# GLA over a whole token group: attention laid out late, by pairs of heads, value rows stored over the values

## The chip, the cores and the metric

The kernel is one launch on one core of a Trainium2 chip. The metric is the device time of that launch in microseconds (us), lower is better. The engines that matter are TensorE (PE, with its weight loads listed as PEld), VectorE (DVE), ScalarE (ACT), GpSimd (POOL) and SyncE (SP, which issues the DMAs). Each engine works through its own instructions strictly in the order in which they stand in the program.

## The reference, cut to what matters

A two-layer decoder trunk runs over 1072 tokens: 16 meta tokens, 8 samples of 4 tokens, and a prompt of 1024. Each layer projects its input once, feeds four mixers of 256 columns each (gated DeltaNet, HGRN2, GLA, retention), projects their concatenation out, normalises, and runs a SwiGLU block. GLA, which the change is about, has 4 heads with 32 key columns and 64 value columns. Per chunk, with `b` the cumulative sum of the log gates:

```python
dec = _masked_exp(b[:, :, None] - b[:, None, :], incl)
att = jnp.einsum('bthk,bshk,btshk->bhts', q, k, dec)
o = (jnp.einsum('bthk,bhkv->bthv', q * jnp.exp(b), s)
     + jnp.einsum('bhts,bshv->bthv', att, v))
s_new = (jnp.exp(b_last)[..., None] * s
         + jnp.einsum('bshk,bshv->bhkv', k * jnp.exp(b_last[:, None] - b), v))
```

HGRN2 uses the same function with 64 key columns. Inputs and outputs are float32.

## The kernel before, in words

Tokens are split into three groups (`GROUPS`): 304 tokens (48 of the lead and two tiles of 128), 384 and 384. A layer has three stages: the input stage (projection of the input, with the four mixers beside it), the output projection, and the feed-forward block.

No order is written by hand. `Kern.run` is a list scheduler that runs while the program is built: a main thread yields the projections, four worker threads yield the mixers' work, and at each step the operation that its cost model places first is emitted. What one thread holds in memory therefore moves the work of all others. Big projections are matmuls of a 128x128 weight tile on 288 to 512 columns, from the tensor R, three for each product. Mixers use small matmuls on parts of the 128x128 array (32x32, 64x64 and so on) from the tensors H and P; each worker has an arena of 3072 columns for its intermediates, two of them in P and two in H. An input of a mixer (`in_begin`) is allocated before its projection and freed by the mixer; when memory is short the main thread waits.

The mixers take tasks from one queue: both DeltaNet pairs for the three groups, then GLA for the three groups, then HGRN2, then retention. A task goes through units (`task_units`). For DeltaNet, HGRN2 and retention these are the lead and the two tiles of group 0, and the three tiles of groups 1 and 2 in one unit. For GLA `HALVES` cuts groups 1 and 2 into a unit of two tiles and one of one tile.

One unit of GLA or HGRN2 is `gated`. It builds the attention matrix level by level (64 and 32 tokens apart, then the levels inside 32: "s8", "s2", "s1" for GLA). A level takes exponentials of differences of `b` (DVE, ACT), small matmuls into a pair of PSUM banks, and copies or predicated copies out. Levels 64 and 32 write into the full attention `at` (128 columns for each head and tile), the inner ones into `ac` (32 columns for each head and tile), whose blocks are copied onto the diagonal of `at` at the end. Then come the rows of keys and values (PE transposes), and `states_and_out`: the state update, the output, and `norm_out`, which normalises with two matmuls of `head_mean` and stores or splits the result. HGRN2 has two heads, so one pair; GLA has two pairs. At the end of a layer's mixers the output projection begins (128x304 or 128x288 matmuls for group 0, 128x512 for groups 1 and 2).

Of the kernel before, what the change touches and what calls it, by code (L numbers as in the profile page):

```python
# [434 lines left out]
class Kern:  # L435
# [1095 lines left out]
    def gated(self, A, l, u, q, k, vs, b, es, K, first, low, upper, S, S0, bo_out, names, sf, spent):  # L1531

        c0, nb, bl = u
        n = nb * bl
# [4 lines left out]
        if lead:  # L1539
            at = A.alloc(H * 48)  # L1540
            yield self.zero(at)
            dst, mrows = at.r("p (h t) -> p h t", h=H), 48
        else:
            at = A.alloc(nb * H * 128)
            yield self.zero(at)
            ac = A.alloc(nb * H * 32)
            yield self.zero(ac)
            dst, mrows = ac.r("p (h x) -> p h x", h=H), 128
        a4 = None if lead else at.r("p (h a t) -> p h a t", h=H, t=128)
        for m in list(first) if lead else list(upper) + list(low):  # L1550
            wk = wq = None
            step = 32
            if m in STEPS:
# [25 lines left out]
            for j in range(H // 2):  # L1579
                bp = self.pair()  # L1580
                prods = []
                for hh in range(2):
                    bk = bp.k(hh)
                    h = 2 * j + hh
                    ks, qs = wk[K * h:K * h + K], wq[K * h:K * h + K]
                    ps = []
                    if lead:
                        ps.append((bk[0:48, 0:48], ks[:, 0:48], qs[:, 0:48]))
                    for a in range(0 if lead else nb):
                        o = 128 * a  # L1590
                        if m == 64:
                            ps.append((bk[0:64, 64 * a:64 * a + 64], ks[:, o:o + 64], qs[:, o + 64:o + 128]))
                        elif m == 32:
                            for z in range(2):
                                ps.append((bk[64 * z:64 * z + 32, 32 * a:32 * a + 32],
                                           ks[:, o + 64 * z:o + 64 * z + 32], qs[:, o + 64 * z + 32:o + 64 * z + 64]))
                        else:
                            for z in range(4):
                                y = step * (4 * a + z)
                                ps.append((bk[32 * z:32 * z + 32, step * a:step * a + step],  # L1600
                                           ks[:, o + 32 * z:o + 32 * z + 32], qs[:, y:y + step]))
                    prods.append(ps)

                for ps in zip(*prods):
                    for x in ps:
                        yield self.mm(*x)
                hs = slice(2 * j, 2 * j + 2)
                if m == 64:
                    yield self.copy2(a4[0:64, hs, :, 64:128], bp[0:64, :, 0:64 * nb].r("p h (a t) -> p h a t", a=nb))
                elif m == 32:  # L1610
                    for z in range(2):
                        r = slice(64 * z, 64 * z + 32)
                        yield self.copy2(a4[r, hs, :, 64 * z + 32:64 * z + 64],
                                         bp[r, :, 0:32 * nb].r("p h (a t) -> p h a t", a=nb))
                elif m in STEPS:
                    yield from self.take_stepped(m, [dst[:, x].r("p (a t) -> p a t", t=32) for x in (2 * j, 2 * j + 1)],
                                                 dst[:, hs].r("p h (a t) -> p h a t", t=32), bp, nb)
                else:
                    nm = (m if isinstance(m, str) else f"l{m}") + ("_0" if lead else "")
                    if lead:  # L1620
                        yield self.pred(dst[0:48, hs], self.mk(nm, 48, 2), bp[0:48, :, 0:48])
                    else:
                        yield self.pred(dst[:, hs].r("p h (a t) -> p h a t", t=32), self.mk4(nm, 2, nb),
                                        bp[:, :, 0:32 * nb].r("p h (a t) -> p h a t", a=nb))
                self.drop(bp)
# [4 lines left out]
        if not lead:  # L1630
            for z in range(4):
                r = slice(32 * z, 32 * z + 32)
                yield self.dcopy(a4[r, :, :, 32 * z:32 * z + 32], dst[r].r("p h (a t) -> p h a t", t=32))
            A.free(ac)
        eb = A.alloc(n)
        yield self.act(AF.Exp, eb, b, scale=es)
        qe = A.alloc(n)
        yield self.tt2(qe, q, eb, MUL)
        ke = A.alloc(n)
        if lead:  # L1640
            yield self.tt2(ke.c(0, 16), b[:, 15:16].bc([128, 16]), b[:, 0:16], SUB)
# [4 lines left out]
            yield self.tt2(ke.r("p (a c) -> p a c", c=128), bv[:, :, 127:128].bc([128, nb, 128]), bv, SUB)  # L1646
        yield self.act(AF.Exp, ke, ke, scale=es)
        yield self.tt2(ke, ke, k, MUL)
        kt = A.alloc(nb * 128)
        A.free(b)  # L1650
        yield from self.rows(ke, nb, bl, [lambda x: iter([self.copy2(kt[0:bl], x[0:bl, 0:nb * 128])])])
        A.free(ke)
        vts = [A.alloc(nb * 128) for _ in vs]
        for v, vt in zip(vs, vts):
            yield from self.rows(v, nb, bl, [lambda x: iter([self.copy2(vt[0:bl], x[0:bl, 0:nb * 128])])])
        self.free(*spent)
        yield from self.states_and_out(A, l, u, qe, kt, vts, at, S, S0, eb, None, K, H, bo_out, names, sf)

    def stepped(self, A, name, q, k, b, es, n):

# [60 lines left out]
            yield self.pred(both, self.mk4("diag", 2, nb), src[:, :, :, 0:32])  # L1721
            yield self.pred(both.r("p h a (i u) -> p h a i u", u=2)[:, :, :, :, 1], self.mk4("s1", 2, nb), src[:, :, :, 32:48])

    def states_and_out(self, A, l, u, qe, kt, vts, at, S, S0, eb, gam, K, H, bo_out, names, sf):

        c0, nb, bl = u
        n = nb * bl
# [13 lines left out]
        else:  # L1741
# [2 lines left out]
                    yield self.mm(bu[K * h:K * h + K, 64 * a:64 * a + 64], kt[:, 128 * a + K * h:128 * a + K * h + K],  # L1744
                                  vv(h, a))
            for a in range(nb):
                sc = gam[0] if gam else eb[:, 128 * a + 127:128 * a + 128]
                yield self.stt(S[a + 1], S[a], sc,
                               bu[:, 64 * a:64 * a + 64], MUL, ADD)
            self.drop(bu)  # L1750
# [6 lines left out]
        for j in range(nv):  # L1757
# [10 lines left out]
            for k in range(2):  # L1768
                for a in range(nb):
                    for hh in range(2):  # L1770
                        h = 2 * j + hh
                        o = bo[64 * hh:64 * hh + 64, bl * a:bl * a + bl]
                        x = h * nb + a
                        if k:
                            r = slice(K * h, K * h + K)
                            yield self.mm(o, S[a][r], qe[r, 128 * a:128 * a + 128], False, a == nb - 1)
                        else:
                            yield self.mm(o, vv(h, a), at[:, 128 * x:128 * x + 128], a == 0, False)
            if j == nv - 1:
                A.free(qe, at, *vts)  # L1780
            yield from bo_out(j, bo)
        if lead:
            yield from self.sample_states(A, l, kt, vts, S0, eb, gam, K, H, names)
# [38 lines left out]

    def task_units(self, A, J, g, state):

        units = (HALVES if J.key[1] == "c" else UNITS)[g]
        mid = A.alloc(64) if g and len(units) == 2 else None
        for k, u in enumerate(units):
            ui = k if g == 0 else g + 1
# [106 lines left out]
    def ret(self, A, l, hh, g, J):  # L1935
# [24 lines left out]
        for x in self.task_units(A, J, g, self.i["sr"][l, hh]):  # L1960
# [41 lines left out]

            if u[0] + n == gn:
                self.free(*ins)
            yield from self.states_and_out(A, l, u, qe, kt, [vt], at, S, S0, None, gam, 64, 2, done,
                                           (None, "rs%d%d" % (l, hh)), sf)
        self.flag(("of", l, 6 + hh, g))

# [644 lines left out]
```

## Time and profile before

| what | value |
| --- | --- |
| median of 3 runs | 3169.23 us (3167.81 to 3171.99) |
| the profiled execution's own time | 3172.53 us |
| its span, first to last instruction | 3170.8 us |
| granted TensorE clock, mean | 0.977 |
| PE busy | 3018.0 us, 95% of the span |
| DVE, ACT, POOL busy | 1731.3, 1111.1 and 529.6 us |
| chain that ended last | PE 65%, DVE 9%, ACT 3%, DMA 2%, issue 2% |

A busy PE is not a PE at its peak: matmuls overlap, and their ends are modelled. So the places where PE is idle or works on small matmuls are read from stretches of the trace, and the pace of the big matmuls from a stretch that holds nothing else. The two input stages lie at about 80 to 640 us and 1640 to 2200 us, each followed by its output projection; the feed-forward blocks fill most of the rest. Fp32 matmuls have two records each in the trace, projections one.

### The profile page before, as it was taken

Reading aid. Unit: us, or ns where it says so; the run is one execution under the profiler, and the core shown is the slowest. Engines: PE = TensorE matmul, PEld = TensorE weight load, DVE = VectorE, ACT = ScalarE, POOL = GpSimd, SP = SyncE. Lnnn points to the kernel's source line nnn. Section 1 sums busy time; section 2 is a strip of 40 time slices with the busy share of each in tenths; the row PEclk is TensorE's granted clock in tenths of the full one; section 3 lists DMA queues with packets and bytes.
Section 4 is the critical chain, followed back from the end, with each engine's and each line's share of the span. In section 5 each row is a group of like instructions: output and inputs, shape, how many; then the busy total and the mean of one; then the engine's idle time right before and its main releaser. Section 6 shows DMA issues by size and latency. Waiting matters only on the chain.

```text
span 3170.8 us, 65772 instructions
## 1 busy us (share of the span) xinstructions
PE 3018.0 (95%) x27758; PEld 2733.2 (86%) x27758; DVE 1731.3 (55%) x3978; ACT 1111.1 (35%) x2310; POOL 529.6 (17%) x617
## 2 busy tenths in 40 slices
PE   7999999989999999999999989999999999999996
PEld 5778887878899999999977778879789999999996
DVE  8886668556633333333497856783774333333336
ACT  5454577432411111111264437763433111111113
POOL 3412213010600000000044211230115000000001
PEclk8999999999999999999999999999999999999998
DMA  5310221241111111111033102123511111111112
GB/s 199 110 49 27 66 64 61 90 158 57 60 54 47 47 40 41 53 47 47 34 125 92 48 26 69 62 65 96 177 47 63 41 40 54 47 47 47 47 40 75
DMA packets 121030, 210.94 MB, mean 67 GB/s; under 512 B 32336, under 2 KB 81488, under 8 KB 120608
## 3 DMA queue, kind: packets, MB, share of 16 engines
q1 hardware_dynamic: 120736, 206.75, 19.7%
q8 instruction: 217, 3.56, 0.5%
q14 instruction: 77, 0.63, 0.1%
HBM read 162.28 MB, written 40.04 MB: 64 GB/s over the span
## 4 chain that ended last, share of the span: by engine, by line
PE 65%; DVE 9%; ACT 3%; DMA 2%; issue 2%; POOL 1%; SPq 0%; DVEq 0%; ACTq 0%; POOLq 0%
PE banks L833 63%; DVE H L864 2%; DVE R L864 2%; DVE H L877 1%; PE banks L839 1%; DVE P L864 1%; ACT H L858 1%; DVE H L902 1%; DVE H L1012 1%; ACT R L855 1%; ACT P L858 1%; ACT L645 0%; DMA H<-XR 0%; DMA H<-OF 0%; POOL H L866 0%
## 5 line engine op out<-in xcount | busy, mean ns | idle before, releaser
L833 PE MATMUL banks<-R 128*128 128x384 f32 (+3 forms) x11840 | 2106.8, 334 | 36.7 <-DVE R L864 13.8
L833 PEld LDWEIGHTS banks<-R 128*128 128x128 f32 x11840 | 1939.0, 191 | 103.9 <-DVE R L864 23.1
L864 DVE TENSOR_TENSOR H<-H,banks 128x512 f32<-128x512 f32 (+6 forms) x722 | 407.3, 568 | 534.6 <-PE banks L833 531.8
L864 DVE TENSOR_TENSOR R<-H,R 128x1024 fp32r<-128x1024 f32 (+5 forms) x356 | 347.8, 987 | 444.6 <-ACT R L855 442.2
L855 ACT CAST R<-H 128x1024 fp32r<-128x1024 f32 (+3 forms) x358 | 284.7, 811 | 803.8 <-PE banks L833 712.0
L833 PE MATMUL banks<-R,P 128*128 128x512 f32 x1584 | 371.7, 394 | 0.0
L833 PEld LDWEIGHTS banks<-R,P 128*128 128x128 f32 x1584 | 296.2, 188 | 66.8 <-issue 0.6
L866 POOL TENSOR_TENSOR H<-H 128x256 f32<-128x256 f32 (+10 forms) x267 | 237.3, 903 | 331.0 <-ACT H L858 81.8
L866 POOL TENSOR_TENSOR P<-H,P 128x384 fp32r<-128x384 f32 (+7 forms) x49 | 73.6, 1503 | 1303.6 <-ACT P L855 1283.4
L858 ACT ACTIVATE H<-H 128x384 f32<-128x384 f32 (+11 forms) x455 | 189.7, 434 | 191.0 <-DVE H L1014 78.9
L833 PE MATMUL banks<-H 32*32 32x32 f32 (+15 forms) x6134 | 203.7, 224 | 22.2 <-issue 8.3
L833 PEld LDWEIGHTS banks<-H 32*32 32x32 f32 (+9 forms) x6134 | 146.8, 121 | 79.5 <-issue 42.8
L833 PE MATMUL banks<-P 32*32 32x32 f32 (+10 forms) x5982 | 170.7, 215 | 26.5 <-DVE P L864 12.4
L833 PEld LDWEIGHTS banks<-P 32*32 32x32 f32 (+6 forms) x5982 | 124.2, 118 | 75.7 <-issue 36.9
L855 ACT COPY H<-banks 128x384 f32<-128x384 f32 (+14 forms) x305 | 112.0, 374 | 219.9 <-PE banks L833 176.6
L855 ACT CAST P<-H 128x304 fp32r<-128x304 f32 (+2 forms) x132 | 64.3, 487 | 284.8 <-DVE H L864 284.8
L864 DVE TENSOR_TENSOR H<-H 128x384 f32<-128x384 f32 (+12 forms) x310 | 131.8, 442 | 50.5 <-ACT H L858 28.9
L858 ACT ACTIVATE H<-banks 128x384 f32<-128x384 f32 (+5 forms) x169 | 72.0, 429 | 228.9 <-PE banks L833 223.5
L839 PE MATMUL banks<-H 128*128 128x128 f32 (+3 forms) x639 | 114.0, 302 | 36.1 <-DVE H L902 16.2
L833 PE MATMUL banks<-P,R 128*128 128x304 f32 (+1 forms) x1056 | 147.4, 299 | 0.0
L833 PEld LDWEIGHTS banks<-P,R 128*128 128x128 f32 x1056 | 145.9, 188 | 0.0
L839 PEld LDWEIGHTS banks<-H 128*128 128x128 f32 (+3 forms) x639 | 77.9, 148 | 69.6 <-DVE H L902 19.0
(86 smaller groups left out, 1714.6 us busy)
## 6 DMA issues: line engine op xcount, KB each, us to landing
H<-in_wst SPq DMA_DIRECT2D x208, 512.0 KB, 3.2
XR<-H SPq DMA_DIRECT2D x12, 512.0 KB, 4.2
GF<-H SPq DMA_DIRECT2D x32, 192.0 KB, 2.2
H<-XR SPq DMA_DIRECT2D x4, 1536.0 KB, 6.7
H<-OF SPq DMA_DIRECT2D x28, 192.0 KB, 4.0
H<-XR SPq DMA_DIRECT2D x41, 128.0 KB, 3.0
XR<-H SPq DMA_DIRECT2D x41, 128.0 KB, 1.8
H<-in_xin SPq DMA_DIRECT2D x8, 512.0 KB, 7.6
```

What stands on the lines that cost most here:

```text
L833: return Op("PE", cost, lambda: self.nc.tensor.matmul(out=out.x(), lhsT=lhsT.ap, rhs=rhs.ap, start=start, stop=stop), (lhsT, rhs), (out,), ...
L839: return Op("PE", 0.83 * p + 2.5, lambda: self.nc.tensor.transpose(out=out.x(), in_=in_.ap, identity=i.ap), (in_,), (out,), 20, None, tile ...
L855: fn = lambda: self.nc.scalar.copy(out=out.x(), in_=in_.x())
L858: fn = lambda: self.nc.scalar.activation(out=out.x(), in_=in_.x(), func=f, scale=s, bias=b)
L864: lambda: self.nc.vector.tensor_tensor(out=out.x(), in0=a.x(), in1=b.x(), op=op), (a, b), (out,))
L866: lambda: self.nc.gpsimd.tensor_tensor(out=out.x(), in0=a.x(), in1=b.x(), op=op), (a, b), (out,), 27.0)
L877: lambda: self.nc.vector.scalar_tensor_tensor(out=out.x(), in0=a.x(), scalar=sc, in1=b.x(), op0=op0, op1=op1),
L902: return Op("DVE", 68 + ptr + rate * out.n, lambda: self.nc.vector.tensor_scalar(out=out.x(), in0=a.x(), **kw), rd, (out,))
L1012: yield Op("DVE", 68 + 1.05 * 512, lambda o=o, s=s: nc.vector.bn_stats(out=o, in_=s.x()), (s,), (st,))
```

## The change

GLA uses the same units as the other mixers, so groups 1 and 2 are one unit of three tiles. To fit the arena, the full attention is allocated only after the inner levels, which now run first, and as one tile for each pair of heads; each is freed as soon as its pair is through. For GLA outside the lead, the transposed value rows are written over the values they came from, whose memory is then freed at the end; `eb` shrinks to its last columns and `qe` takes its place. HGRN2 shares `gated`, so its levels change order too; retention only wraps its attention in a list.

```diff
@@ gated
-            at = A.alloc(nb * H * 128)
-            yield self.zero(at)
             ac = A.alloc(nb * H * 32)
             yield self.zero(ac)
             dst, mrows = ac.r("p (h x) -> p h x", h=H), 128
-        a4 = None if lead else at.r("p (h a t) -> p h a t", h=H, t=128)
-        for m in list(first) if lead else list(upper) + list(low):
+        for m in list(first) if lead else list(low) + list(upper):
+            if not lead and m == upper[0]:
+                at = [A.alloc(nb * 256) for _ in range(H // 2)]
+                for x in at:
+                    yield self.zero(x)
+                a4 = [x.r("p (h a t) -> p h a t", h=2, t=128) for x in at]
...
-                yield self.dcopy(a4[r, :, :, 32 * z:32 * z + 32], dst[r].r("p h (a t) -> p h a t", t=32))
+                for j, x in enumerate(a4):
+                    yield self.dcopy(x[r, :, :, 32 * z:32 * z + 32],
+                                     dst[r, 2 * j:2 * j + 2].r("p h (a t) -> p h a t", t=32))
             A.free(ac)
         eb = A.alloc(n)
         yield self.act(AF.Exp, eb, b, scale=es)
-        qe = A.alloc(n)
-        yield self.tt2(qe, q, eb, MUL)
+        if lead:
+            qe = A.alloc(n)
+            yield self.tt2(qe, q, eb, MUL)
+        else:
+            eb, qe = A.alloc(nb), eb
+            yield self.dcopy(eb, qe.r("p (a c) -> p a c", c=128)[:, :, 127])
+            yield self.tt2(qe, q, qe, MUL)
...
-        vts = [A.alloc(nb * 128) for _ in vs]
+        place = not lead and len(vs) > 1
+        vts = vs if place else [A.alloc(nb * 128) for _ in vs]
...
-        self.free(*spent)
+        self.free(*(spent[:-len(vs)] if place else spent))
@@ states_and_out
-                sc = gam[0] if gam else eb[:, 128 * a + 127:128 * a + 128]
+                sc = gam[0] if gam else eb[:, a:a + 1]
...
-                            yield self.mm(o, vv(h, a), at[:, 128 * x:128 * x + 128], a == 0, False)
+                            yield self.mm(o, vv(h, a), at[j][:, 128 * x:128 * x + 128], a == 0, False)
+            A.free(at[j])
             if j == nv - 1:
-                A.free(qe, at, *vts)
+                A.free(qe, *(() if place else vts))
+                if place:
+                    self.free(*spent[-len(vts):])
@@ task_units
-        units = (HALVES if J.key[1] == "c" else UNITS)[g]
+        units = UNITS[g]
```

What this does to the order of PE's instructions is shown at three places. In the rows, `banks` is PSUM, R holds projections and their weights, H and P the mixers' data, and the last numbers are the output's partitions and columns and how many such matmuls stand together.

First, PE in layer 0, at GLA's inner levels (32x48 matmuls). Before, a unit of two tiles, and further down a unit of one tile:

```order
L833 MATMUL banks<-H 32x48 x32
L833 MATMUL banks<-R 128x384 x14
L833 MATMUL banks<-H 32x48 x32
L833 MATMUL banks<-R 128x48 x2
L833 MATMUL banks<-R 128x384 x12
L833 MATMUL banks<-H 32x48 x32
...
L833 MATMUL banks<-P_74 32x48 x16
L833 MATMUL banks<-R 128x304
L833 MATMUL banks<-R 128x384 x18
L833 MATMUL banks<-R 128x48 x2
L833 MATMUL banks<-R 128x384 x13
L833 MATMUL banks<-P_74 32x48 x16
```

Now the same place, with the three tiles of a group in one burst:

```order
L833 MATMUL banks<-H 32x48 x48
L833 MATMUL banks<-R 128x48 x2
L833 MATMUL banks<-R 128x384 x11
L833 MATMUL banks<-H 64x48 x2
L833 MATMUL banks<-H 64x4 x16
L833 MATMUL banks<-R 128x384 x18
L833 MATMUL banks<-H 32x48 x48
L833 MATMUL banks<-R 128x384 x11
L833 MATMUL banks<-R 128x48 x2
L833 MATMUL banks<-R 128x384 x4
L833 MATMUL banks<-H 32x48 x48
```

Bursts of 32 and of 16 have become one of 48, and the separate bursts of 16 are gone from the order further down.

Second, PE in layer 1, where DeltaNet's triangular inverses (32x32) of two workers stand, before GLA. Before:

```order
L833 MATMUL banks<-H 32x32 x12
L833 MATMUL banks<-P_14795 64x64 x48
L833 MATMUL banks<-P_14795 32x32 x16
L833 MATMUL banks<-H 32x32 x24
L833 MATMUL banks<-H 128x128 x6
L833 MATMUL banks<-H,P_14795 128x64
L833 MATMUL banks<-P_14795 32x32 x16
L833 MATMUL banks<-H 32x32 x24
L833 MATMUL banks<-H 64x64 x45
L833 MATMUL banks<-P_14795 32x32 x16
L833 MATMUL banks<-H 32x32 x24
L833 MATMUL banks<-H 64x64 x3
```

Now the same place, by the number of projection matmuls that stand ahead of it:

```order
L833 MATMUL banks<-P_14617 64x64 x48
L833 MATMUL banks<-P_14617 32x32 x8
L833 MATMUL banks<-H 32x32 x24
L833 MATMUL banks<-R 128x304 x8
L833 MATMUL banks<-P_14617 32x32 x8
L833 MATMUL banks<-H 32x32 x24
L833 MATMUL banks<-R 128x304 x6
L833 MATMUL banks<-P_14617 128x128 x4
L833 MATMUL banks<-H 32x32 x24
L833 MATMUL banks<-R 128x304 x6
L833 MATMUL banks<-P_14617 64x64 x32
L833 MATMUL banks<-H 32x32 x24
```

Projection matmuls (R) now stand between the small ones, where before 235 small matmuls stood together.

Third, PE at the end of layer 0's input stage: the last retention unit (64x64 x6 and 64x128 x12 from H, then `head_mean`, 128x384 from R) and the output projection around it. Before:

```order
L839 MATMUL banks<-H 128x128 x6
L833 MATMUL banks<-H 128x128 x6
L833 MATMUL banks<-H 64x64 x6
L833 MATMUL banks<-R 128x512 x14
L833 MATMUL banks<-H 64x128 x12
L833 MATMUL banks<-R 128x512 x7
L833 MATMUL banks<-R 128x384 x2
L833 MATMUL banks<-R 128x512 x11
L833 MATMUL banks<-R 128x384 x2
L833 MATMUL banks<-R 128x512 x4
L833 MATMUL banks<-R 128x304 x48
L833 MATMUL banks<-R 128x512 x72
```

Now:

```order
L833 MATMUL banks<-R 128x304 x48
L833 MATMUL banks<-R 128x512 x18
L839 MATMUL banks<-H 128x128 x6
L833 MATMUL banks<-H 128x128 x6
L833 MATMUL banks<-R 128x512 x3
L833 MATMUL banks<-H 64x64 x6
L833 MATMUL banks<-R 128x512 x6
L833 MATMUL banks<-H 64x128 x12
L833 MATMUL banks<-R 128x512 x7
L833 MATMUL banks<-R 128x384 x2
L833 MATMUL banks<-R 128x512 x11
L833 MATMUL banks<-R 128x384 x2
```

The last unit stood in the first pass of the output projection and now stands in the second, behind its 48 matmuls of group 0. In layer 1 it moved the other way, from the second pass into the first.

## Rows read from the trace of the kernel before

**Rows 1.** The page: span, and each engine's busy time, share, instructions.

```profile
span 3170.8 us, 65772 instructions
PE 3018.0 (95%) x27758; PEld 2733.2 (86%) x27758; DVE 1731.3 (55%) x3978; ACT 1111.1 (35%) x2310; POOL 529.6 (17%) x617
```

**Rows 2.** Windows: length; busy PE, PEld, DVE, ACT, POOL (instructions); PEclk, DMA share, GB/s.

```profile
80.00:640.00 560.00, 527.44 (x8134) 455.60 (x8133) 389.24 (x1143) 304.12 (x699) 131.97 (x200) 0.98 0.22 68
1640.00:2200.00 560.00, 521.53 (x8064) 454.09 (x8064) 381.20 (x1152) 301.12 (x696) 139.29 (x205) 0.97 0.21 65
840.00:1560.00 720.00, 720.00 (x4185) 688.90 (x4185) 250.88 (x369) 122.95 (x190) 57.78 (x39) 1.00 0.13 47
```

**Rows 3.** The chain that ended last (start us, us, what): layer 0's feed-forward block.

```profile
838.59 732.70 PE banks L833 x4266
```

**Rows 4.** Timeline of PE, layer 0: start us, us, instruction, records, [idle].

```profile
307.06 1.32 PE L833 MATMUL banks<-R 128*128 128x384 f32 x6
308.31 0.62 PE L833 MATMUL banks<-P 32*32 32x32 f32 x48
308.86 0.30 PE L833 MATMUL banks<-H 32*48 32x48 f32 x8
309.09 1.33 PE L833 MATMUL banks<-R 128*128 128x384 f32 x6
310.35 0.94 PE L833 MATMUL banks<-P 32*32 32x32 f32 x80
311.21 1.14 PE L833 MATMUL banks<-R 128*128 128x384 f32 x5
```

**Rows 5.** The same view, GLA's inner levels: two tiles, one tile.

```profile
358.10 0.80 PE L833 MATMUL banks<-H 32*32 32x48 f32 x64
428.91 0.37 PE L833 MATMUL banks<-P 32*32 32x48 f32 x32
```

**Rows 6.** Windows as in rows 2, over GLA's units in either layer.

```profile
280.00:520.00 240.00, 225.87 (x3378) 192.42 (x3377) 165.95 (x539) 149.77 (x376) 55.19 (x95) 0.96 0.18 57
1880.00:2080.00 200.00, 194.34 (x2544) 169.15 (x2540) 133.37 (x465) 134.20 (x327) 42.92 (x75) 1.00 0.19 61
```

**Rows 7.** Groups by form: count | busy us, mean ns of one | idle before, releaser.

```profile
L864 DVE TENSOR_TENSOR H<-H 128x384 f32<-128x384 f32 x81 | 46.1, 584 | 18.6 <-DMA H<-H 11.1 <-ACT H L858 4.9 <-PE banks L833 1.3
L864 DVE TENSOR_TENSOR H<-H 128x256 f32<-128x256 f32 x45 | 20.8, 462 | 10.6 <-ACT H L858 5.4 <-PE banks L833 4.8
L864 DVE TENSOR_TENSOR H<-H 128x128 f32<-128x128 f32 x48 | 13.5, 297 | 3.7 <-ACT H L858 3.5
L858 ACT ACTIVATE H<-H 128x384 f32<-128x384 f32 x161 | 81.8, 520 | 32.1 <-DVE H L864 15.0 <-DVE H L877 12.7 <-DVE H L902 1.6
L858 ACT ACTIVATE H<-H 128x256 f32<-128x256 f32 x38 | 15.6, 414 | 6.9 <-DVE H L864 4.0 <-DVE H L907 2.4
L858 ACT ACTIVATE H<-H 128x128 f32<-128x128 f32 x39 | 11.4, 307 | 9.2 <-POOL H L866 4.4 <-DVE H L864 3.0 <-DVE H L907 1.6
L645 ACT ACT_TABLE_LOAD x98 | 125.7, 1283 | 1.7
L927 POOL MEMSET H<- 128x768 f32 x13 | 9.6, 739 | 36.3 <-PE banks L833 36.2
```

**Rows 8.** Layer 1's dense stretch: window; PE's waits (total us, times, longest).

```profile
1800.00:1880.00 80.00, 67.75 (x2096) 58.28 (x2086) 50.01 (x148) 21.85 (x56) 14.46 (x21) 0.96 0.07 20
PE banks L833 <- issue: 7.9, 7, 2.2
```

**Rows 9.** Windows as in rows 2: the ends of the two input stages.

```profile
640.00:720.00 80.00, 66.38 (x421) 55.64 (x420) 49.49 (x97) 31.12 (x66) 14.32 (x13) 0.87 0.47 149
2200.00:2280.00 80.00, 75.68 (x533) 65.48 (x532) 49.84 (x103) 32.81 (x70) 8.65 (x11) 1.00 0.56 183
```

More of the change, by code (lines that the diff above doesn't have):

```diff
@@ L1608, in gated @@
                 if m == 64:
-                    yield self.copy2(a4[0:64, hs, :, 64:128], bp[0:64, :, 0:64 * nb].r("p h (a t) -> p h a t", a=nb))
+                    yield self.copy2(a4[j][0:64, :, :, 64:128], bp[0:64, :, 0:64 * nb].r("p h (a t) -> p h a t", a=nb))
                 elif m == 32:
@@ L1612, in gated @@
                         r = slice(64 * z, 64 * z + 32)
-                        yield self.copy2(a4[r, hs, :, 64 * z + 32:64 * z + 64],
+                        yield self.copy2(a4[j][r, :, :, 64 * z + 32:64 * z + 64],
                                          bp[r, :, 0:32 * nb].r("p h (a t) -> p h a t", a=nb))
@@ L1648, in gated @@
         yield self.tt2(ke, ke, k, MUL)
+        A.free(b)
         kt = A.alloc(nb * 128)
-        A.free(b)
         yield from self.rows(ke, nb, bl, [lambda x: iter([self.copy2(kt[0:bl], x[0:bl, 0:nb * 128])])])
         A.free(ke)
-        vts = [A.alloc(nb * 128) for _ in vs]
+        place = not lead and len(vs) > 1
+        vts = vs if place else [A.alloc(nb * 128) for _ in vs]
         for v, vt in zip(vs, vts):
             yield from self.rows(v, nb, bl, [lambda x: iter([self.copy2(vt[0:bl], x[0:bl, 0:nb * 128])])])
-        self.free(*spent)
-        yield from self.states_and_out(A, l, u, qe, kt, vts, at, S, S0, eb, None, K, H, bo_out, names, sf)
+        self.free(*(spent[:-len(vs)] if place else spent))
+        yield from self.states_and_out(A, l, u, qe, kt, vts, at, S, S0, eb, None, K, H, bo_out, names, sf, place, spent)
     def stepped(self, A, name, q, k, b, es, n):
@@ L1722, in take_stepped, with states_and_out @@
             yield self.pred(both.r("p h a (i u) -> p h a i u", u=2)[:, :, :, :, 1], self.mk4("s1", 2, nb), src[:, :, :, 32:48])
-    def states_and_out(self, A, l, u, qe, kt, vts, at, S, S0, eb, gam, K, H, bo_out, names, sf):
+    def states_and_out(self, A, l, u, qe, kt, vts, at, S, S0, eb, gam, K, H, bo_out, names, sf, place=False, spent=()):
         c0, nb, bl = u
@@ L1772, in states_and_out @@
                         o = bo[64 * hh:64 * hh + 64, bl * a:bl * a + bl]
-                        x = h * nb + a
+                        x = hh * nb + a
                         if k:
@@ L2004, in ret @@
                 self.free(*ins)
-            yield from self.states_and_out(A, l, u, qe, kt, [vt], at, S, S0, None, gam, 64, 2, done,
+            yield from self.states_and_out(A, l, u, qe, kt, [vt], at if lead else [at], S, S0, None, gam, 64, 2, done,
                                            (None, "rs%d%d" % (l, hh)), sf)
```

## The prediction, made before the changed kernel ran

> **What bounds the kernel now.** I read the page first, then the windows of the stages, then the chain. The page says PE: 3018.0 of 3170.8 us busy, DVE 1731.3, ACT 1111.1 [rows 1]. That average hides two kinds of stage. In a feed-forward block PE has no gap at all (720.00 of 720.00 us, clock 1.00), and the chain runs through it as one piece of 4266 matmuls in 732.70 us, 0.172 us each [rows 2, 3]. Nothing of the change lies there. In the two input stages PE is busy 527.44 and 521.53 of 560 us, so idle 32.6 and 38.5 us, and the clock is 0.98 and 0.97 [rows 2]. DVE is busy 389 and 381 us of the 560 (70%), ACT 304 and 301. So even beside the mixers PE is the fullest engine, and its waits are short gaps between bursts, not one engine's backlog. What the change can win is three things: PE's own work, the price of going between big and small matmuls, and a share of these 71 us. The reader is to see that the mixers' work on DVE, ACT and POOL counts only where PE waits for it.
>
> **PE's own work.** The three-tile unit does the same small matmuls for each tile. The rows agree: an inner level of two tiles takes 0.80 us for 64 records and one of one tile 0.37 us for 32 [rows 5], so the pair costs 1.17 us; at the same 12 ns a record, 96 records cost about 1.2. No gain there. What goes is `head_mean`: ten units of more than the lead become six over both layers (five and three in each), with four matmuls each, so 16 matmuls fewer in 21462. Their columns stay (256 + 128 against 384), so I set this at nothing; the work that takes its place is the wider matmul itself, and without that it would be at most 16 times 0.172, 2.8 us.
>
> **Going between big and small.** In the timeline of PE, six projection matmuls between two bursts take 1.25 us from start to start (307.06 to 308.31) and again 1.26 (309.09 to 310.35) [rows 4]. At 0.172 each they would take 1.03, so 0.22 us is lost. The burst behind them: 48 records from 308.31 to 308.86 are 0.55 us, 80 records from 310.35 to 311.21 are 0.86 us, so 9.7 ns a record and 0.08 us fixed [rows 4]. One burst put among projections thus costs 0.30 us beyond its work. Counted over the whole order, runs of matmuls on part of the array fall from 351 to 336, since the one-tile bursts join the two-tile ones: 15 times 0.30, 4.6 us less. The ends are 0, if an idle gap takes the place of each, and 6.9, if each also frees as much again half.
>
> The Trainium skill, TensorEngine Tiling (Array Packing), section "Key Properties", says that changing the tiling mode drains TensorE and gives no price, while its section "PSUM Bottleneck" says that small tiles speed up TensorE but not the evacuation of PSUM, so that the copies out may become the bound. By the first, the 4.6 us above is real; by the second, it is not where the gain is, and the copies decide, which is the second rival below.
>
> **DVE, ACT and POOL.** Counted over the order, and net of what is added: DVE loses 155 instructions, ACT 123 (127 fewer, 4 table loads more), POOL 38. A pair of 256 and 128 columns against one of 384 costs DVE 462 + 297 - 584 = 175 ns more, ACT 414 + 307 - 520 = 201 ns [rows 7]. That is 27 us off DVE and 25.5 off ACT, less 4 x 1.283 = 5.1 us of table loads, so 20. These are beside PE's work nearly everywhere. Where they reach PE is over GLA's units: PE idles 240 - 225.87 = 14.1 us in layer 0 and 200 - 194.34 = 5.7 in layer 1 [rows 6], 19.8 together. GLA's units fall by four in ten, so at most 7.9 us can go if all of that idle time were GLA's. DeltaNet and HGRN2 run there too, so I take half, 4 us; the lower end is 0.
>
> **What is added and moved.** The attention's zeroing on POOL comes late: 0.74 us for 768 columns [rows 7], twice for a GLA unit, once for an HGRN2 unit. It is issued ahead of the chain of level 64 (a subtraction, two exponentials and two products, on 384 columns at 0.52 to 0.58 us each [rows 7], so over 2.5 us), and that hides it. Behind it on POOL stand only shares of the same work, which DVE can take as well. If the cover is gone, 24 such memsets at 0.74 us would be 18 us on the mixers' chain, and PE would see the share that it sees of other mixer time: the 71 us of idle time over 770 us of DVE work in the two stages [rows 2], a tenth, so under 2 us. The 18 small copies of the last column and the doubled diagonal copies are in the net count above. In retention nothing moves but names. The stores and loads of `norm_out` fall by 18 on SP's queue, and nothing is queued behind them that PE waits for. Value rows in the values' place hold the inputs longer, to the end of the output instead of the transposes. But before, all inputs of a group were held until its second unit was through, and that one stood far down (428.91 us for its first inner burst against 358.10 for the first unit's [rows 5]). So I expect memory to come free earlier, not later.
>
> **The new plan around it.** The scheduler places everything after the first GLA task anew. Two places matter.
>
> In layer 1, where two workers' inverses meet, PE idles 80 - 67.75 = 12.3 us in 80, and for 7.9 us of these, 7 times, it waits for nothing that the profile shows ("issue"), in the densest runs of small matmuls [rows 8]. In the order before, the fullest stretch of 20 projection matmuls has 362 small ones beside it there, now 208. In layer 0 the fullest near the first GLA task has 204 now where 100 stood, but the order before has stretches that full in layer 0 as well (236). I take half of the 7.9 us, 4, as gone; the ends are 8 gained and 2 lost.
>
> At the ends of the input stages PE idles 80 - 66.38 = 13.6 us at clock 0.87 in layer 0, and 4.3 us at 1.00 in layer 1 [rows 9]. The order shows that the two layers trade shapes here: layer 0's last retention unit goes from the first pass of the output projection into the second, where layer 1's stood, and layer 1's goes the other way. If the shape makes the gap, one layer gains what the other loses; if the place does (its weights and stores), nothing changes. Either way I set the sum at 0, with ends at one layer's difference: 13.6 - 4.3 = 9.3 us of idle time, plus the clock. A mean of 0.87 is 26% of the 80 us at 1.2 GHz, in which half the work is done, so up to 10.4 us. Together 19.7 us either way.
>
> **Sum.** -4.6 (bursts) - 4 (GLA's gaps) - 4 (dense stretch) + 0 (ends) = -12.6 us. From the profiled execution's 3172.53 us (span 3170.8 and 1.7 around it) this is 3159.9. The median of the runs before is 3.3 us below that execution, so for the median 3156.6, which I give as 3157.
>
> **Rivals.**
>
> *The mixers set the pace.* If PE's gaps came from DVE's backlog, all 27 us of DVE would count beside the 4.6, in place of the two terms of 4: 31.7 us, or 3137 for the median. For it speaks that DVE is 70% busy in the input stages; against it, that PE is at 94% there and DVE never full [rows 2, 6]. Here the skill's page named above would put the bound; the rows show PE fuller than DVE in both of GLA's windows (225.87 against 165.95, 194.34 against 133.37), so it gets little.
>
> *Layer 1 takes layer 0's end, and layer 0 keeps its own.* The head means of the last units then stand among the first output matmuls in both layers, PE waits for them in order, and the clock falls as in rows 9. That costs 19.7 us against the 12.6 gained: 3176. It decides as soon as the new gap is above 12.6 us. For it speaks the trade of shapes; against it, that layer 0's shape goes as well, and with it the most likely cause.
>
> *Nothing comes of it.* The list scheduler fills each freed slot, the joined bursts only move the same waits to the next place, and gaps of 8 us are what two plans of equal worth differ by. Then only part of the 4.6 us shows: 3165 to 3169. For it speaks that all added slack is on engines that are not the bound; against it, that the burst price is paid by PE itself.
>
> **How the numbers follow.** The forecast has a chance of 0.5, with a range of its own from 3148 (both middle terms at their upper ends, 7.9 and 8) to 3165 (both at 0). The faster mixers have 0.13, the worse end of layer 1 0.17, nothing 0.2. A measurement of this kernel tells about 0.2%, 6.3 us, from no change, so faster is below 3162.9 and slower above 3175.6. Faster: 0.43 of the forecast's 0.5, the 0.13, and 0.02 of the nothing case, 0.58. Slower: 0.1 of the 0.17, and some 0.06 from plans that lose elsewhere by as much, 0.16. The rest, 0.26, is the same. The range runs from the faster mixers at 3137 to the worse end with 2 us of the late memsets on top, 3178.
>
> **What would show it.** In the profile after, PE's windows over GLA should have under 16 us of idle time, the busy time of DVE and ACT in the input stages some 10 us less in each layer, the inner levels bursts of 96 records at about 1.2 us, and the waits for "issue" in layer 1's dense stretch half. I am wrong if the feed-forward stretches change, if the two ends of the input stages add up to much more or less than 18 us of idle time, or if the clock in them falls in both layers.

## The result, and the profile after

The changed kernel took 3134.5 us in the median of four executions (3125.1 to 3135.6), the kernel before 3170.6 beside it: a ratio of 0.988, interval 0.986 to 0.990. Six more executions later (e9), on another chip and beside other kernels, gave 0.9902 (0.9880 to 0.9923), some 31 us. So the change is worth 31 to 36 us; forecast were 12.6, and the range missed the first median by 2.5 us.

The page of the changed kernel: span, then busy time, share and instructions of each engine, as in [rows 1].

```profile
span 3132.8 us, 65384 instructions
PE 2993.8 (96%) x27742; PEld 2722.0 (87%) x27742; DVE 1727.6 (55%) x3823; ACT 1098.3 (35%) x2187; POOL 514.7 (16%) x579
```

PE is 24.2 us less busy and 13.8 less idle. DVE issues 155 instructions fewer, as counted, but its busy time falls by 3.7 us only, where 27 were forecast; ACT loses 12.8, POOL 14.9.

Windows of the changed kernel over the stretches of [rows 2, 6, 9], moved with the program in layer 1: length; busy PE, PEld, DVE, ACT, POOL with instructions; PEclk, DMA share, GB/s.

```profile
80.00:640.00 560.00, 526.89 (x8142) 462.31 (x8141) 384.45 (x1064) 291.24 (x634) 125.65 (x178) 0.97 0.22 68
840.00:1560.00 720.00, 720.00 (x4204) 688.73 (x4203) 255.34 (x383) 124.34 (x190) 39.83 (x26) 1.00 0.14 47
280.00:520.00 240.00, 225.92 (x3453) 198.64 (x3451) 167.06 (x461) 147.17 (x325) 52.50 (x80) 0.98 0.19 60
1860.00:2060.00 200.00, 190.88 (x2825) 170.87 (x2823) 142.61 (x399) 136.78 (x286) 42.72 (x65) 1.00 0.21 66
640.00:720.00 80.00, 74.15 (x488) 61.47 (x487) 58.10 (x109) 32.06 (x66) 13.44 (x14) 0.98 0.55 176
2150.00:2230.00 80.00, 71.00 (x508) 63.09 (x505) 46.69 (x98) 33.28 (x71) 10.14 (x10) 0.94 0.52 163
```

The feed-forward block is untouched (720.00 of 720.00 again). Over GLA's units PE idles 14.1 and 9.1 us, 23.2 together, not less than the 19.8 of before, but it gets through more in the same time (3453 matmul records for 3378, 2825 for 2544). The two ends have traded: layer 0's has 5.9 us idle at clock 0.98, layer 1's 9.0 at 0.94.

A window of fixed length holds different work in two kernels. So I cut both programs at the same projections (the head means' matmuls left out, both have 14256): from number 200 to 2200 is layer 0's input stage, to 3000 its end; 7200 to 9200 and to 10000 the same in layer 1. First the kernel before.

```profile
87.80:690.90 603.10, 560.67 (x8346) 485.48 (x8345) 413.53 (x1187) 322.54 (x738) 138.13 (x200) 0.97 0.25 76
690.90:881.20 190.30, 180.51 (x1040) 157.12 (x1040) 120.77 (x201) 61.10 (x113) 58.18 (x46) 0.96 0.21 70
1631.10:2225.30 594.20, 554.19 (x8279) 485.35 (x8279) 400.15 (x1209) 310.51 (x721) 145.14 (x214) 0.97 0.22 67
2225.30:2418.30 193.00, 181.24 (x1121) 156.18 (x1120) 140.09 (x246) 75.19 (x149) 59.83 (x49) 0.98 0.29 98
```

The changed kernel, the same four pieces of work.

```profile
84.20:676.10 591.90, 554.15 (x8336) 486.53 (x8335) 404.69 (x1101) 309.41 (x672) 132.67 (x183) 0.97 0.25 77
676.10:860.50 184.40, 176.33 (x1039) 153.75 (x1039) 126.31 (x209) 61.81 (x114) 56.78 (x46) 0.99 0.23 75
1609.40:2181.90 572.50, 540.67 (x8272) 475.75 (x8272) 401.88 (x1135) 309.47 (x661) 132.15 (x191) 0.99 0.23 69
2181.90:2380.20 198.30, 182.41 (x1119) 158.15 (x1118) 139.49 (x243) 76.04 (x151) 61.54 (x50) 0.97 0.30 96
```

Layer 0's input stage gives 11.2 us (4.7 of them idle time), layer 1's 21.7 (8.2 idle), layer 0's end 5.9, and layer 1's end costs 5.3. PE's busy time also falls, by 6.5 and 13.5 us in the two stages. Part of that is the clock: layer 1's stage was granted 0.97 before and 0.99 after. This part is chance of the two executions shown and not of the change. Over 22 executions of the kernel before the mean granted clock is 0.9819, over the six of e9 0.9827; in the profiled one of before it was 0.977.

To keep chance and plan apart, the table below has, in us and for these four pieces together, the idle time of PE, the time that the clock took (one less the granted clock, times the length), and what is left, PE's own work at full clock. Cut are the kernel before and e1, e3, e12; whole are the changed kernel (mean of its two profiles), e2, e4, e11, all described below.

| us | time | idle | clock | own work |
|---|---|---|---|---|
| before | 1580.5 | 104.0 | 47.8 | 1428.7 |
| changed (two profiles) | 1547.8 | 93.5 | 36.7 | 1417.6 |
| mean of four cut | 1574.6 | 105.6 | 38.8 | 1430.2 |
| mean of four whole | 1554.4 | 97.4 | 39.5 | 1417.5 |

Whole groups have 12.7 us less of PE's own work and 8.2 less idle time, and no better clock.

### The profile page after: what moved, and what is told of

The parts are those of the page before. It is cut to its first block, busy times and chain, and to the rows that moved or that the text cites. A ratio compares the mean times of both kernels' runs of the same rounds, so it can differ in the third digit from the quotient of the medians.

```text
span 3132.8 us, 65384 instructions
## 1 busy us (share of the span) xinstructions
PE 2993.8 (96%) x27742; PEld 2722.0 (87%) x27742; DVE 1727.6 (55%) x3823; ACT 1098.3 (35%) x2187; POOL 514.7 (16%) x579
## 5 line engine op out<-in xcount | busy, mean ns | idle before, releaser
L833 PE MATMUL banks<-R 128*128 128x384 f32 (+2 forms) x11824 | 2094.1, 333 | 26.0 <-DVE H L877 10.0
L864 DVE TENSOR_TENSOR H<-H,banks 128x512 f32<-128x512 f32 (+5 forms) x713 | 403.4, 570 | 528.6 <-PE banks L833 525.6
L864 DVE TENSOR_TENSOR R<-H,R 128x1024 fp32r<-128x1024 f32 (+4 forms) x348 | 348.2, 1011 | 438.5 <-ACT R L855 436.4
L866 POOL TENSOR_TENSOR P<-H,P 128x384 fp32r<-128x384 f32 (+6 forms) x49 | 73.2, 1495 | 1292.3 <-ACT P L855 1282.2
L866 POOL TENSOR_TENSOR H<-H 128x256 f32<-128x256 f32 (+7 forms) x230 | 213.9, 945 | 264.4 <-ACT H L858 83.1
L833 PE MATMUL banks<-H 32*32 32x32 f32 (+13 forms) x5560 | 185.3, 225 | 26.2 <-DVE H L864 11.3
L833 PE MATMUL banks<-P 32*32 32x32 f32 (+12 forms) x6404 | 171.8, 212 | 23.1 <-DVE P L864 8.4
L833 PEld LDWEIGHTS banks<-P 32*32 32x32 f32 (+7 forms) x6404 | 129.3, 117 | 70.5 <-issue 35.8
L855 ACT COPY H<-banks 128x384 f32<-128x384 f32 (+11 forms) x278 | 107.0, 391 | 186.6 <-PE banks L833 155.5
L858 ACT ACTIVATE H<-banks 128x384 f32<-128x384 f32 (+5 forms) x166 | 71.1, 430 | 231.5 <-PE banks L833 224.4
L864 DVE TENSOR_TENSOR H<-H 128x384 f32<-128x384 f32 (+13 forms) x283 | 130.9, 480 | 29.9 <-ACT H L858 17.4
L839 PE MATMUL banks<-H 128*128 128x128 f32 (+4 forms) x636 | 110.0, 295 | 36.9 <-DVE H L902 14.5
```

The costliest lines, as they stand in the source:

```text
L833: return Op("PE", cost, lambda: self.nc.tensor.matmul(out=out.x(), lhsT=lhsT.ap, rhs=rhs.ap, start=start, stop=stop), (lhsT, rhs), (out,), ...
L839: return Op("PE", 0.83 * p + 2.5, lambda: self.nc.tensor.transpose(out=out.x(), in_=in_.ap, identity=i.ap), (in_,), (out,), 20, None, tile ...
L855: fn = lambda: self.nc.scalar.copy(out=out.x(), in_=in_.x())
L858: fn = lambda: self.nc.scalar.activation(out=out.x(), in_=in_.x(), func=f, scale=s, bias=b)
L864: lambda: self.nc.vector.tensor_tensor(out=out.x(), in0=a.x(), in1=b.x(), op=op), (a, b), (out,))
L866: lambda: self.nc.gpsimd.tensor_tensor(out=out.x(), in0=a.x(), in1=b.x(), op=op), (a, b), (out,), 27.0)
```

## The experiments

Fifteen runs follow, of which e9 is the changed kernel again. All ratios are against runs of the kernel before on the same chip, with a 95% interval; 0.1% is 3.2 us.

**Units or layout?** e1 is the changed kernel with GLA's groups cut again.

```diff
-        units = UNITS[g]
+        units = (HALVES if J.key[1] == "c" else UNITS)[g]
```

> The changed kernel with one line put back: GLA's groups 1 and 2 are again a unit of two tiles and one of one tile; late attention by pairs, level order and value rows in place stay. Units theory (the joined bursts and the fewer gaps of whole groups are the gain): most of the 36 us is lost, 3160 to 3172. Layout theory (order of levels, late attention, memory): it stays below 3145. Plan theory (any new order of the scheduler lands some 10 to 20 us up or down): anything from 3130 to 3170, with no relation to the number of bursts.

0.9997 (0.9980 to 1.0014). With the groups cut, all of the gain is gone, so it hangs on the units; the new layout with cut groups is neither gain nor loss. Its page shows what moved between the engines.

```profile
PE 3003.8 (95%) x27758; PEld 2720.6 (86%) x27758; DVE 1747.9 (55%) x4055; ACT 1096.5 (35%) x2301; POOL 529.8 (17%) x611
```

Against before, the layout puts 16.6 us on DVE and takes 14.6 off ACT. The whole groups then take 20.3 off DVE and 15.1 off POOL, and leave ACT as it is. The forecast had put both into one sum.

**The order of the levels.** e2 lets HGRN2 keep its upper levels first (`late` is true for GLA alone).

```diff
-        for m in list(first) if lead else list(low) + list(upper):
+        late = len(vs) > 1
+        for m in list(first) if lead else (list(low) + list(upper) if late else list(upper) + list(low)):
```

> The changed kernel with HGRN2's levels in their old order (64 and 32 first, attention allocated before them); GLA as changed. Units theory: as the changed kernel, 3125 to 3142, since nothing of GLA's units moves. Layout theory: 5 to 15 us of the gain go, 3140 to 3150. Plan theory: 3120 to 3150, by chance.

0.9938 (0.9915 to 0.9961), 3146 us in the median and so outside the 3125 to 3142 of the units theory. Some 12 us of the changed kernel's gain hang on it or on the plan that came with it. Which of the two this run can't tell.

**How far do plans scatter?** e3 and e12 are the kernel before, e4 and e11 the changed one, each with one number of the scheduler altered.

```diff
-HOLD, SLACK = 600.0, 150.0
+HOLD, SLACK = 600.0, 200.0   # e3, e4
+HOLD, SLACK = 650.0, 150.0   # e11, e12
```

> The kernel before with one number of the scheduler changed that does no work of its own (its dislike of going back from small to big matmuls, SLACK, 150 to 200). Units theory: 3160 to 3180. Plan theory: more than 10 us away from 3170, either way; a run at 3150 or below would mean that a redrawn plan alone can give half of the gain.

> The changed kernel with the same number changed (SLACK 150 to 200). Units theory: 3125 to 3145, so that the distance to the kernel before with the same number stays at 25 us or more. Plan theory: more than 10 us away from 3134, either way, and the distance to the kernel before with the same number below 15 us.

> The changed kernel under another plan (the wait that the scheduler puts on a first small matmul 650 for 600). With e2 and e4 a third sample of how far plans of whole groups scatter. If whole groups are worth 0.9% or so by themselves, 0.988 to 0.995; if the changed kernel was a lucky plan, 0.997 to 1.003.

> The kernel before with the same 650 for 600, a sample of how far plans of cut groups scatter, besides e1 and e3 (0.9997 and 1.0000). If the cut itself costs, 0.997 to 1.003 again; if plans scatter by a per cent, anything from 0.990.

Cut groups: e3 1.0000 (0.9988 to 1.0011), e12 0.9969 (0.9953 to 0.9984), with e1 and the kernel itself a mean of 0.9992. Whole groups: e4 0.9915 (0.9888 to 0.9943), e11 0.9922 (0.9893 to 0.9951), with e2 and 0.9902 a mean of 0.9919. None of these plans of whole groups is as slow as the fastest of cut ones, though the intervals of e2 and e12 touch. With the same numbers in the scheduler the distance is 31 us (the kernels themselves, by e9), 27 (e3 to e4) and 15 (e12 to e11). So the units are worth 0.7%, 23 us, by the scatter of four plans of either kind some 8 us more or less. The 8 to 13 us beyond that belong to this pair of plans; why it is a better pair stays open.

**Part of the units.** e6 cuts the second group only, e7 both groups in layer 1 only, e8 cuts both groups into three single tiles.

```diff
+        units = (HALVES if J.key[1] == "c" and g == 1 else UNITS)[g]             # e6
+        units = (HALVES if J.key[1] == "c" and J.key[0] == 1 else UNITS)[g]      # e7
+        units = (THIRDS if J.key[1] == "c" else UNITS)[g]                        # e8
```

> The changed kernel with GLA's second group cut again into two tiles and one, the third left whole. If each joined group is worth the same by itself (bursts and head means), half of the gain stays: ratio about 0.994. If the gain is a matter of where two plans happen to fall, it is anywhere from 0.988 to 1.000, and the pieces of the program in which it gains are others than in the changed kernel. If the second group alone makes it: 1.000.

> The changed kernel with GLA's groups cut again in layer 1 only; up to layer 1 the program is the changed kernel's to the row. Theory, each layer pays for itself: layer 0 keeps its 10 us in the input stage and 11 us at its end, layer 1 is as before, ratio about 0.9935. Rival, layer 1's gain comes from a better start left by layer 0 (the plan's clocks): layer 1 keeps its 17 us too and the ratio is 0.988 to 0.990.

> The changed kernel with GLA's second and third group cut into three units of one tile each: twice as many extra units as the halves had. If the price of a cut is per unit (bursts, head means, the short waits beside them), the distance doubles: halves lay 1.2% above the whole groups, so thirds lie about 2.4% above them, ratio to before 1.01, some 3197. If only the joined burst counts and halves already had most of it, or the gain was the accident of one plan, it is 0.997 to 1.003.

e6: 1.0025 (1.0012 to 1.0039), no half of the gain. Cut into the same pieces, its input stages take 597.7 and 584.0 us, 5.4 and 10.2 less than before. But in the execution shown the clock took 7.7 and 12.0 us less there than in that of before, so without it they are 2.3 and 1.8 longer, and layer 1's end takes 208.8 where before took 193.0. e7: 0.9991 (0.9975 to 1.0007). Layer 0 keeps its gain (585.4 us for the input stage, 188.1 for the end; without the clock's share the stage is 575.2, 573.8 in the changed kernel and 583.5 before). Layer 1 is back at 591.7 (579.8 without the clock's share, 564.0 changed, 577.1 before), and its end takes 204.1. e8: 1.0157 (1.0130 to 1.0183), with 618.9 and 615.9 us in the stages (12 and 13 above before without the clock's share) and 209.6 in layer 1's end. So in e7 and e8 each layer's input stage pays for its own units, and what a plan then does at layer 1's end can take it all back. The simple dose that I expected fell in e6, where one whole group of two gives the stages nothing; in e8 it came out above the 1.01 expected.

**What is time on DVE and ACT worth?** Four kernels carry extra instructions on a scratch tile, of which the plan knows nothing; PE's order is that of the kernel they start from. In e5 and e10 one and two products stand behind each masked copy of GLA's levels s2 and s1, in e13 three exponentials behind each of the stepped levels'. In e14, which is the kernel before, one narrower product stands behind each masked copy of level s2 alone.

```diff
     self.nc.vector.copy_predicated(out=out.x(), mask=mask, data=data.x())
+    self.nc.vector.tensor_tensor(out=self.X[:, :], in0=self.X[:, :], in1=self.X[:, :], op=MUL)
```

> The changed kernel with 96 extra products on DVE (128x112 on a scratch tile, 16 in each GLA unit beyond the lead, right behind the masked copies of levels s2 and s1), of which the plan knows nothing, so PE's order is unchanged to the row. At some 0.28 us each (a product of 128 columns took 297 ns) DVE does 27 us more, as much as the forecast had the change take off it. If DVE sets the pace of the mixers (first rival), all of it comes back: ratio to before about 0.997, some 3160. If PE's own work and order made the gain and DVE's time is covered, a tenth shows: 2 to 4 us, ratio 0.988 to 0.990.

> The changed kernel with the load on DVE doubled: 192 products of 112 columns, 56 us, PE's order unchanged. If DVE sets the pace, the time rises by nearly all of it: ratio about 1.005. If a third of DVE's time shows at PE, 18 us above the changed kernel: 0.994 to 0.998, and the rise lies in the input stages alone. If its time is covered up to a point, the second 28 us cost clearly more than the first.

> The changed kernel once more, beside the next ones on one chip, to take their ratios from the same runs. If its 0.988 stands, the load of 28 us on DVE gave back some 25 us (0.9961 against 0.988) and DVE's time counts nearly in full; if it comes out at 0.991 to 0.993, the load gave back 10 to 15 us, a third to a half, as its profile says (span 9.7 us longer).

> The changed kernel with 90 extra exponentials on ACT (128x112 on a scratch tile, three behind each exponential of GLA's stepped levels beyond the lead), unknown to the plan, PE's order unchanged. At some 0.29 us each that is 26 us, beside the 20 that the forecast had the change take off ACT. If every engine of the mixers' chain counts, as DVE does (28 us gave back 19), 12 to 20 us come back: ratio 0.994 to 0.997. If DVE alone is the one that PE waits for, ACT's time is covered: 0.989 to 0.992.

> The kernel before with 120 extra products of 80 columns on DVE behind the masked copies of level s2, about 27 us, PE's order unchanged. If DVE's time counts in full in the cut plan, as the second 28 us did in the changed kernel, the ratio is about 1.008; with two thirds of it, 1.006; and then the 18 us that the change took off DVE's sum explain 12 to 18 of the gain. If the cut plan is bound by PE's own gaps and DVE is covered, 1.000 to 1.002, and the gain isn't DVE's.

The load that was added, in e5, e10, e13 and e14 in this order: count | busy us, mean ns | idle before.

```profile
L917 DVE TENSOR_TENSOR X<-X 128x112 f32<-128x112 f32 x96 | 28.0, 292 | 0.0
```

```profile
L918 DVE TENSOR_TENSOR X<-X 128x112 f32<-128x112 f32 x192 | 53.3, 278 | 3.3
```

```profile
L920 ACT ACTIVATE X<-X 128x112 f32<-128x112 f32 x90 | 26.3, 293 | 1.9
```

```profile
L917 DVE TENSOR_TENSOR X<-X 128x80 f32<-128x80 f32 x120 | 29.6, 247 | 0.0
```

e5: 0.9961 (0.9947 to 0.9975) against e9's 0.9902, so 19 us for 28.0 on DVE. e10: 1.0059 (1.0041 to 1.0077), 50 us for 53.3, the second load in full. e13: 0.9951 (0.9936 to 0.9965), 15 us for 26.3 on ACT. e14: 1.0054 (1.0039 to 1.0069), 17 us for 29.6 on DVE in the kernel before. These engines are at 55% and 35% by the page, and yet a microsecond more in GLA's chain costs 0.6 of one, on DVE in the cut plan as in the whole one, and on ACT in the whole one; past some 28 us on DVE it costs all of it. These differences have 5 us (e14) to 9 us (e10) of error either way. By the pages, the engines' own busy time rises by less than the load (21.1, 45.6, 21.4 and 24.7 us), so 0.6 to 0.9 is as near as these runs tell it for the first 28 us.

How PE loses it under the double load is seen in the two input stages, first of e9, then of e10.

```profile
80.50:664.80 584.30, 548.73 (x8337) 481.63 (x8336) 404.58 (x1100) 308.49 (x671) 131.21 (x182) 0.98 0.25 77
1599.40:2179.00 579.60, 546.79 (x8271) 481.41 (x8271) 403.91 (x1135) 309.42 (x661) 131.76 (x193) 0.97 0.23 69
```

```profile
81.50:695.90 614.40, 566.06 (x8337) 494.50 (x8336) 426.51 (x1197) 309.62 (x672) 130.39 (x184) 0.95 0.24 74
1631.80:2233.40 601.60, 558.53 (x8271) 488.21 (x8271) 426.89 (x1231) 309.51 (x661) 131.06 (x191) 0.95 0.22 66
```

The stages take 52.1 us more. Idle time is less than half of it: 35.6 and 32.8 us become 48.3 and 43.1, together 23.0 more. The other 29.1 are PE's busy time, which rises for the same matmuls, with the granted clock down from 0.98 and 0.97 to 0.95 and 0.95. Over all executions of e10 the mean granted clock is 0.9740, over those of e9 0.9827, which is 28 of the 50 us. Under a single load it is a small part: e14 was granted 0.9808 and the kernel before beside it 0.9820, 4 us of its 17.

PE's waits in e10's first input stage (engine and line waited for: us, times, longest) name the loaded chain. L916 is the masked copy with the products behind it, L866 the products of all mixers.

```profile
PE banks L835 <- DVE P L866: 7.8, 9, 2.4
PE banks L835 <- DVE H L866: 7.4, 9, 2.3
PE banks L835 <- DVE H L916: 5.4, 7, 1.8
PE banks L835 <- DVE P L916: 2.4, 1, 2.4
```

In e9 the same products make it wait 10.5 us (6.2 and 4.3), the masked copies not at all. Here it is 23.0.

**Moving work from DVE to ACT.** e15 puts 96 copies of the diagonal blocks on ACT.

```diff
-                    yield self.dcopy(x[r, :, :, 32 * z:32 * z + 32],
+                    yield self.act(AF.Copy, x[r, :, :, 32 * z:32 * z + 32],
```

> The changed kernel with its 96 copies of the diagonal blocks into the attention put on ACT in place of DVE: 29 us less on DVE, about as much more on ACT (which is 35% busy, DVE 55%). A new plan, so some 5 us of scatter. If DVE's time alone is the price, it is 10 to 19 us faster than the changed kernel: ratio 0.984 to 0.987. If ACT stands in the same chain, nothing is won: 0.989 to 0.993.

0.9975 (0.9962 to 0.9989), slower than the changed kernel by 23 us, more than either theory gave. DVE's busy time falls by 14.2 us against e9, ACT's rises by 17.9, so by the loads nothing should be won. The loss is most of all idle time in layer 0's input stage, 46.7 us for 35.6. Whether that is ACT's longer queue or another plan's luck, this run leaves open. No version beat the changed kernel.

## Why the prediction was wrong, point by point

The step of the sum that failed is PE's own work beside the bursts, which was set at nothing and gave 7.0 us. The argument failed in the price of time on DVE and ACT. And the 8 to 13 us that this pair of plans adds had no place in the sum.

**Bounds and feed-forward: right.** Of the 38.0 us between the two profiles 33.5 lie in the input stages and their ends, as said; 3.6 more lie ahead of the first piece, where starts scatter (84.2 for 87.8 us, and 80.5 in e9).

**Bursts, 4.6 us: right, partly by luck.** Sorted by what stands ahead of it, a projection behind a burst of small matmuls adds 0.365 us to PE's busy time, one behind another projection 0.171. Of the first kind the four cut plans have 231.5 on average, the whole ones 208: 23.5 times 0.194, 4.6 us. The forecast came to the same with other factors, 15 times 0.30.

**The work inside bursts, "no gain there", and `head_mean`, "at nothing": the terms that were mis-sized on PE.** For the inner levels the prediction was right: 1.17 us for a two-tile and a one-tile burst, and about 1.2 for one of 96 records. The timeline of the changed kernel has (start us, us):

```profile
319.22 1.19 PE L833 MATMUL banks<-P,H 32*32 32x48 f32 x96
363.63 1.11 PE L833 MATMUL banks<-H 32*32 32x48 f32 x96
```

All their matmuls (32x48) take 17.5 us in either family. But over all small matmuls of the four pieces whole plans have 4.4 us less than cut ones (289.9 for 294.3), most of it in three other forms (128x128 on 64 columns of the array 1.5 us, 32x128 1.3, 32x32 1.1); what shortens these no run shows. The head means have 2.6 less (45.6 for 48.3), nearly the 2.8 that the prediction gave as its upper end. It took neither into the sum. With the bursts these three make 11.6 of the 12.7 us of PE's own work in the table.

**GLA's gaps and layer 1's dense stretch, 4 us each: right together, less so apart.** Idle time fell by 8.2 us between the families and by 10.5 between the two kernels. In the fixed windows over GLA it rose, 23.2 for 19.8, and the test "under 16" failed. But those windows hold more work now. Between the projections that [rows 6] lie between, the changed kernel has:

```profile
278.90:506.20 227.30, 215.54 (x3301) 189.78 (x3300) 155.77 (x442) 137.96 (x302) 46.23 (x72) 0.98 0.19 60
1831.10:2042.60 211.50, 205.31 (x3234) 181.80 (x3233) 147.99 (x438) 136.17 (x292) 40.67 (x68) 1.00 0.20 62
```

That is 18.0 us idle, 2 to 3 less than before, and still not under 16. The dense stretch gave more, at the upper end of its term. A window of the same length over it, and PE's waits for "issue" in it, beside [rows 8]:

```profile
1770.00:1850.00 80.00, 75.75 (x2124) 65.34 (x2113) 55.25 (x168) 37.21 (x83) 14.84 (x24) 1.00 0.09 26
PE banks L833 <- issue: 1.6, 2, 1.2
```

Idle 4.3 us for 12.3, "issue" 1.6 for 7.9. That is the plan's doing more than the units'. Between the projections of [rows 8] the changed kernel, e7 and e11 have:

```profile
1778.70:1831.10 52.40, 49.39 (x1425) 43.16 (x1414) 34.09 (x97) 25.36 (x53) 7.39 (x10) 1.00 0.05 13
1779.80:1831.40 51.60, 49.20 (x1424) 43.07 (x1415) 34.00 (x97) 25.42 (x53) 7.39 (x11) 1.00 0.05 13
1788.70:1858.80 70.10, 60.40 (x1816) 53.20 (x1815) 42.05 (x131) 19.98 (x49) 10.71 (x17) 0.93 0.07 20
```

With fewer small matmuls between the same projections (1425 records in all) the stretch is gone, in e7 as well, whose layer 1 has cut groups; and it is there in e11 (9.7 us idle), whose groups are whole. Little of it reaches the whole of layer 1's input stage: that has 31.8 us idle here, but 39.7 in e2, where the stretch is gone too, 36.6 in e4 and 40.8 in e11. The cut plans have 40.0 (before), 45.3 (e1), 43.2 (e3) and 45.4 (e12), so whole groups do save some 6 us there.

**"These are beside PE's work nearly everywhere": the step of the argument that failed.** The prediction granted PE a tenth of the mixers' time (71 us idle over 770 of DVE), and about as little of the 47 us of relief. The loads measure six tenths or more, and all of it past some 28 us. A ratio of two totals says nothing on what one more microsecond does, and under the double load more than half of the price came as a lower clock, not as idle time. That the term still came out near its size is an accident of two errors: DVE's relief was counted as 27 us, from durations of instructions that overlap, and with the layout in the same sum; its busy time fell by 3.7. By e1's page the units alone free 20.3 us of DVE, but e1 is the plan with the most of it (1747.9; e3 and e12 have 1729.7 and 1737.5). Over the two families of the table the units free 5.1 us of DVE and 10.6 of ACT, which at 0.6 would be 9 us, against the 8.2 of idle time seen. No run takes this relief alone, so that last step is argued, not shown. The test "DVE and ACT some 10 us less in each stage" failed too: DVE has 8.8 us less and 1.7 more, ACT 13.1 and 1.0 less.

**Ends, 0: right.** Layer 0 gains 5.9 us, layer 1 loses 5.3, the trade that the order showed; in the windows of [rows 9] they idle 14.9 us together, for 17.9. The plan decides it more than the units: e12, with cut groups, has 184.6 and 192.5 us.

**What is left.** The units are worth 20 us in the table and 23 by the ratios; the forecast had 12.6. The other 8 to 13 us of the result the prediction had only as "gaps of 8 us are what two plans of equal worth differ by", and gave them no place in the sum. They are of that size, and fell on the good side: that part of the result is luck, and no run shows what in the plan gives it.

**The rivals.** The faster mixers (the first of the three, called the second above) came nearest in time (3137), but not as told: DVE was not relieved by 27 us, and PE's own work made more than the waits (12.7 us for 8.2). Layer 1 did take a worse end, for 5.3 us, with layer 0's gain beside it. That nothing comes of it is ruled out by the four plans of whole groups.

## What to carry to other kernels

Price time on an engine beside the bound one by what a microsecond more on it does, and not by its share: a load that the plan does not know, in an unchanged order, measures it in one run, for the place where it stands. Take a small term that has a bound on one side only into the sum at half of it: the head means, set at nothing, came out at 2.6 us of at most 2.8. And before a gain of a scheduled kernel is explained, time two or three neighbouring plans of either kind: here they scatter by 0.3 to 0.4%, a third of the gain.

## What the runs showed of the hardware

In stretches where PE is busy for 94% with short gaps, more waiting can cost more than its length: under e10's double load 23.0 us more idle time came with 29.1 us more busy time for the same matmuls, at a mean granted clock lower by 0.02 to 0.03. Under single loads that did not show: in the four pieces of e14 idle time rose by 12.4 us, and the clock took 3.4 less. In GLA's chain ACT, at 35% of the span, is no more covered than DVE at 55%: some 0.6 us for each one added. The full-array matmul behind a burst on part of the array adds 0.19 us more to PE's busy time than its like in every profile (0.36 to 0.37 for 0.17).
